# Exponentials issued behind the copies of B, two banks for the samples' transposes, and their decays loaded early, in a pooling and SSD step

## The chip, the cores and the metric

The kernel runs on one core of a Trainium2 chip. The metric is the time of one execution on the device, in microseconds (us). The core has five engines with a queue of instructions each: TensorE (PE, matmuls), VectorE (DVE), ScalarE (ACT), GpSimd (POOL) and SyncE (SP, which here issues nearly all DMAs). Each engine works through its own queue in order; what waits at the head of a queue holds all behind it. PEld is the loading of weights into PE, which overlaps its matmuls.

## The reference

One inference step of two layers, x = x + mixer(RMSNorm(x)), for a prompt of 1024 tokens and for eight sample requests of eight tokens with carried states. Layer 0 is a gated mixer of pooling windows, layer 1 a Mamba-2 mixer (SSD) with 32 heads of 64 in four groups, state size 128 and chunks of 128 tokens. The change is in layer 1, whose scan is:

```python
a = dt * A                                # per head
a_cum = cumsum(a, within the chunk of 128)
L = exp(where(causal, a_cum_i - a_cum_j, -inf))
CB = einsum('bcign,bcjgn->bcgij', C, B)   # B, C are shared by the 8 heads of a group
W = CB * L * dt
y_diag = einsum('bcgeij,bcjgep->bcigep', W, x)
decay_to_end = exp(a_cum_last - a_cum) * dt
chunk_states = einsum('bcjgn,bcgej,bcjgep->bcgepn', B, decay_to_end, x)
h = exp(a_cum_last) * h + chunk_states    # from chunk to chunk
y_off = einsum('bcign,bcgepn,bcgei->bcigep', C, h_before_chunk, exp(a_cum))
y = y_diag + y_off + D * x, gated by silu(z), normed, projected
```

## The kernel before

Everything is computed in fp32. A weight is split into a high and a low part (`whi`, `wlo`), an activation too, and three matmuls stand for one: high by high, low by high, high by low. The 1024 prompt tokens and the 64 sample tokens are worked in two halves h of 512 + 32 = 544 columns, and each product in two column halves of 272. So nearly all of PE's work is a row of 128x128 by 128x272 matmuls in `product` (line 172), 24 for a tile of 128 outputs of the input projections, into one of three PSUM banks `big`. ACT casts a weight to its high part (line 155); the low part comes by DMA or from DVE. Weights have two raw buffers and three of each part.

In layer 1 the four groups g of a half follow each other. While a group is worked, the projections, convolutions and gates of the same and of the next group supply the large matmuls among which its small ones are set. For a group:

- `ssd_common`: for each of four chunks c, PE transposes B (line 607) and multiplies C by B (608) into one bank of `tr` (two banks, used by many others too), and ACT copies both out: the product to `bs` (610), the transpose to `bt` (612).
- `sample_common`, `sample_states`: for the 32 sample tokens, eight small matmuls with C as the weight multiply the carried states (723, 32 rows each) into the bank `of`; ACT copies the result (725). For each quad q of four heads PE transposes it into `of` again (730; `of` is one bank), a DMA brings the decays `bEs` (734, one tile), and DVE multiplies the two into `ys` (737).
- `ssd`, for each quad q: for each chunk a DMA brings the decays `bA` (641, two tiles), POOL masks them (642), ACT takes four exponentials into `L` (646, four tiles), DVE multiplies them by `bs` (647); PE transposes x (650), DVE scales it to `xd` and `xs` (654), PE multiplies by `L` into `dg` (660). In the second half the state of the first comes in: PE multiplies it by C into `of` (674).
- `ssd_sample`: the same for the sample tokens, ending in a new state `hs` (775).
- the convolution of a tile: ACT copies u out of `big` (184), starts it (578), DVE adds three terms (580), ACT takes the tanh (592), DVE finishes it (593, 597).

When the first half is done, its closing norms are worked among the first group of the second half: PE sums squares over partitions (205), DVE scales (213), ACT takes the square root (214), DVE makes the reciprocal and one refining step (215 to 218), and PE spreads the result to all partitions (225).

The order on each engine is not the order of the code. The kernel is built with a scheduler that plays a timeline at build time and sets each engine's queue by when it believes inputs to be ready, within dependences; `tc.high_priority()` lifts a block in it. So an edit at one place can move rows on every queue.

Of the kernel before, what the change touches and what calls it, by code (L numbers as in the profile page):

```python
# [9 lines left out]
F32 = mybir.dt.float32  # L10
F32R = mybir.dt.float32r
AF = mybir.ActivationFunctionType
# [4 lines left out]
P = 128  # L17
# [8 lines left out]
NB = 4  # L26
LS = 8
SM = NB * LS
# [48 lines left out]
def pool_ssd_step(ctx, tc, xin, spool, sconv, sssm, w_pin, w_mix, w_pout, w_sin, w_dt, w_sout, params, consts,  # L77
                  y_out, pool_p, pool_s, conv_p, conv_s, ssm_p, ssm_s):
    nc = tc.nc
    V, S, G, PE = nc.vector, nc.scalar, nc.gpsimd, nc.tensor  # L80
# [4 lines left out]
    sp = ctx.enter_context(tc.tile_pool(name="sp", bufs=1))  # L85
    big = ctx.enter_context(tc.tile_pool(name="big", bufs=3, space=PSUM))
    sps = ctx.enter_context(tc.tile_pool(name="sps", bufs=1, space=PSUM))
# [385 lines left out]
    esd = [dp.tile([NH, SM], F32, name=f"esd{h}") for h in range(2)]  # L473
# [90 lines left out]
    def conv_part(h, act, g, j):  # L564
# [33 lines left out]
                               op0=ALU.add, op1=ALU.mult)  # L598
        return xpair[0] if j < 4 else o

    def ssd_common(B, C):

        out = []
        for c in range(NCH):
            cs = slice(c * Q, (c + 1) * Q)
            pb = sps.tile([P, 2, NS], F32, name="tr", bufs=2)
            PE.transpose(pb[:, 0], B[:, cs], ident)
            PE.matmul(pb[:, 1], B[:, cs], C[:, cs], start=True, stop=True)
            bs = sp.tile([P, 1, NS], F32, name="bs", bufs=NCH)
            S.copy(bs, pb[:, 1:])  # L610
            bt = sp.tile([P, NS], F32, name="bt", bufs=NCH)
            S.copy(bt, pb[:, 0])
            out.append((bs, bt))
        return out

    def heads(x):
        return x.rearrange("p (e d) -> p e d", e=4)
# [4 lines left out]
    def by_head(x, i):  # L622

        return x[:, i:i + 4, None].broadcast_to([x.shape[0], 4, HD])

    def ssd(h, g, q, x, ys, C, com, nat, cdb):
# [5 lines left out]
        for c0 in range(0, NCH, 2):  # L632
# [3 lines left out]
            for c in (c0, c0 + 1):  # L636
                cs = slice(c * Q, (c + 1) * Q)
                ci = c * NH + h0

                bA = sp.tile([P, 4, Q], F32, name="bA", bufs=2)  # L640
                nc.sync.dma_start(out=bA, in_=acd[h][c:c + 1, h0:h0 + 4].broadcast_to([P, 4, Q]))
                G.affine_select(out=bA, in_=bA, pattern=[[0, 4], [1, Q]], compare_op=ALU.is_ge, fill=-1e30, base=0,
                                channel_multiplier=-1)
                L = sp.tile([P, 4, Q], F32, name="L", bufs=4)
                for e in range(4):
                    S.activation(out=L[:, e], in_=bA[:, e], func=AF.Exp, bias=nat[:, 0, ci + e:ci + e + 1])  # L646
                V.tensor_tensor(out=L, in0=L, in1=com[c][0].broadcast_to([P, 4, Q]), op=ALU.mult)
                px = sps.tile([P, 2 * P], F32, name="tr", bufs=2)
                for k in range(2):
                    PE.transpose(px[:, k * P:(k + 1) * P], x[:, k, cs], ident)  # L650
                xd = sp.tile([P, 2 * P], F32, name="xd", bufs=2)
                xs = sp.tile([P, 2 * P], F32, name="xs", bufs=2)
                for k, x1 in enumerate((xd, xs)):
                    V.tensor_tensor(out=heads(x1), in0=heads(px), in1=by_head(nat[:, 1 + k], ci), op=ALU.mult)
                xds.append(xd)
                xss.append(xs)
                Ls.append(L)
# [5 lines left out]
            po = sps.tile([P, 2, 2 * Q], F32, name="of")  # L663
            bE = sp.tile([P, 2, 2 * Q], F32, name="bE")
            for n in range(2):
                c = c0 + n
                cs = slice(c * Q, (c + 1) * Q)
                ns = slice(n * Q, (n + 1) * Q)
                if hf is not None:
                    ev = ecd[h][c:c + 1, h0:h0 + 4].rearrange("c (k r) i -> c r k i", r=2)  # L670
# [41 lines left out]
    def sample_states(h, g, C):  # L712

        ss = slice(LP, T)
        states = []

        pn = sps.tile([P, 2, 2 * P], F32, name="of")
        for q in range(2):
            hs = sp.tile([P, NB, 2 * P], F32, name="hs", bufs=2)
            nc.sync.dma_start(out=hs, in_=sssm[h, g, q].rearrange("b p f -> p b f"))  # L720
            states.append(hs)
            for b in range(NB):
                PE.matmul(pn[b * SM:(b + 1) * SM, q], C[:, ss], hs[:, b], start=True, stop=True)
        yn = sp.tile([P, 2, 2 * P], F32, name="bE")
        S.copy(yn, pn)
        outs = []
        for q in range(2):
            po = sps.tile([P, 2, NB, SM + LS], F32, name="of")
            for k in range(2):
                PE.transpose(po[:, k].rearrange("p b i -> p (b i)")[:, :P], yn[:, q, k * P:(k + 1) * P], ident)  # L730
            bE = sp.tile([P, 2, SM], F32, name="bEs")
            ev = esd[h][None, g * 8 + q * 4:g * 8 + q * 4 + 4].rearrange("c (k r) i -> c r k i", r=2)
            for r in range(2):
                nc.sync.dma_start(out=bE[r * 64:(r + 1) * 64], in_=ev[:, r].broadcast_to([64, 2, SM]))
            ys = sp.tile([P, 2, T], F32, name="ys", bufs=2)

            V.tensor_tensor(out=by_seq(ys[:, :, ss]), in0=po[:, :, :, :LS], in1=by_seq(bE), op=ALU.mult)
            outs.append(ys)
        return states, outs
# [366 lines left out]
```

## Time and profile before

| | us |
|---|---|
| median of three runs | 1576.95 (1576.25 to 1577.57) |
| the profiled execution | 1577.91 |
| its span | 1575.8 |

The profiled execution is 0.96 us above the median; 2.11 us of it lie outside the span, which runs from the first recorded instruction to the last. PE is busy nearly all the time; the granted clock of TensorE is 0.994 of full on the mean. A reader looks for three things in such a profile: where PE stood idle and what ended it, in which windows its clock was below full, and what the other engines had in their queues at that time. Layer 1 starts in earnest at 703 us, where PE comes to the first group of the first half; the first group of the second half comes at 1129 us.

### The profile page before, as it was taken

What the parts mean: (1) busy time and instruction counts of PE and PEld (TensorE: products, weight loads), DVE (VectorE), ACT (ScalarE), POOL (GpSimd) and SP (SyncE); (2) the same over time, 40 slices, a digit from 0 to 9 for tenths busy, and PEclk for the clock granted to TensorE, in tenths of its full rate; (3) what the DMA queues carried; (4) which work ended last, traced back from release to release, by engine and by line L of the source; (5) the groups of instructions that cost most, each with busy time, mean ns of one, the idle gap of its engine ahead of it and who ended that gap; (6) DMA issues with size and microseconds to landing.
All of it is one profiled execution on the core that took longest, in us unless ns stands there. A gap on an engine that the chain in (4) does not pass through costs nothing.

```text
span 1575.8 us, 32628 instructions
## 1 busy us (share of the span) xinstructions
PE 1551.3 (98%) x12636; PEld 1514.5 (96%) x12636; DVE 1078.8 (68%) x2019; ACT 735.1 (47%) x1462; POOL 318.7 (20%) x516
## 2 busy tenths in 40 slices
PE   9999999999999999999999999999999999999996
PEld 8999999999999999998999999999999899999996
DVE  6787778865557576658666476577678864865757
ACT  5553433545343434355555554543645555535422
POOL 2200000003101011015432132222323521322310
PEclk9999999999999999999999999999999999999998
DMA  7856556758555556554846657656667576475563
GB/s 260 256 183 195 199 177 207 256 181 279 180 182 177 187 173 207 163 182 142 271 152 210 212 164 214 227 171 237 199 186 253 198 214 213 163 237 190 180 219 116
DMA packets 163210, 315.77 MB, mean 200 GB/s; under 512 B 33392, under 2 KB 71408, under 8 KB 163056
## 3 DMA queue, kind: packets, MB, share of 16 engines
q1 hardware_dynamic: 162768, 313.42, 61.8%
q8 instruction: 99, 1.62, 0.4%
q14 instruction: 55, 0.45, 0.1%
q10 hardware_dynamic: 288, 0.28, 0.1%
HBM read 262.47 MB, written 51.16 MB: 199 GB/s over the span
## 4 chain that ended last, share of the span: by engine, by line
PE 85%; DVE 5%; DMA 5%; ACT 1%; POOL 1%; issue 1%; SPq 1%; DVEq 0%; POOLq 0%; ACTq 0%
PE big L172 75%; PE dg L660 2%; PE stt L676 2%; PE of L674 1%; DVE win L580 1%; DMA bA<-acd 1%; DMA L<-in_w_sin_dram 1%; PE tr L650 1%; DMA bE<-ecd 1%; PE big L392 1%; DMA bEs<-esd 1%; PE stt L774 0%; DMA d<-d 0%; DMA low<-bA 0%; DVE X L888 0%
## 5 line engine op out<-in xcount | busy, mean ns | idle before, releaser
L172 PE MATMUL big<-ah,whi 128*128 128x272 f32 (+1 forms) x2304 | 667.1, 290 | 0.5 <-DVE X L428 0.5
L172 PE MATMUL big<-al,whi 128*128 128x272 f32 (+1 forms) x2304 | 666.9, 289 | 0.0
L172 PE MATMUL big<-ah,wlo 128*128 128x272 f32 (+1 forms) x2304 | 666.4, 289 | 0.0
L172 PEld LDWEIGHTS big<-ah,whi 128*128 128x128 f32 (+1 forms) x2304 | 432.1, 188 | 5.7 <-ACT bs L610 2.1
L172 PEld LDWEIGHTS big<-ah,wlo 128*128 128x128 f32 (+1 forms) x2304 | 432.7, 188 | 1.3 <-issue 0.4
L172 PEld LDWEIGHTS big<-al,whi 128*128 128x128 f32 (+1 forms) x2304 | 432.5, 188 | 1.0 <-issue 0.3
L155 ACT CAST whi<-raw 128x1024 fp32r<-128x1024 f32 (+1 forms) x228 | 237.8, 1043 | 361.1 <-PE big L172 272.6
L172 PE MATMUL big<-y,whi 128*128 128x272 f32 x2016 | 392.3, 291 | 2.2 <-DVE X L813 1.2
L172 PEld LDWEIGHTS big<-y,whi 128*128 128x128 f32 x2016 | 317.9, 188 | 5.6 <-DVE X L813 1.4
L172 PE MATMUL big<-y,wlo 128*128 128x272 f32 x1008 | 293.5, 291 | 0.0
L157 DVE TENSOR_TENSOR wlo<-raw,whi 128x1024 fp32r<-128x1024 f32 x112 | 138.6, 1238 | 87.8 <-ACT whi L155 86.3
L172 PEld LDWEIGHTS big<-y,wlo 128*128 128x128 f32 x1008 | 190.4, 189 | 0.7 <-issue 0.4
L580 DVE SCALAR_TENSOR_TENSOR win<-u,par,win 128x556 f32<-128x556 f32 x144 | 123.3, 857 | 43.7 <-ACT win L578 41.6
L646 ACT ACTIVATE L<-bA,nat 128x128 f32<-128x128 f32 x256 | 79.9, 390 | 47.3 <-PE dg L660 36.1
L141 ACT CAST bA<-L 128x512 fp32r<-128x512 f32 (+1 forms) x113 | 69.9, 619 | 62.7 <-DMA L<-in_w_sin_dram 34.6
L142 DVE TENSOR_TENSOR bA<-L,bA 128x512 fp32r<-128x512 f32 (+1 forms) x113 | 78.0, 691 | 27.5 <-ACT bA L141 25.0
L172 PE MATMUL big<-p,whi 128*128 128x272 f32 x512 | 96.7, 288 | 0.0
L172 PEld LDWEIGHTS big<-p,whi 128*128 128x128 f32 x512 | 80.3, 188 | 0.0
L331 POOL COPY uc<-u 128x15 f32<-128x15 f32 x30 | 22.3, 742 | 258.7 <-ACT u L184 169.2
L184 ACT COPY u<-big 128x272 f32<-128x272 f32 (+2 forms) x192 | 52.6, 309 | 46.0 <-PE big L172 35.3
L428 DVE TENSOR_TENSOR X<-X,big 128x272 f32<-128x272 f32 x128 | 54.5, 432 | 28.4 <-PE big L172 28.2
L172 PE MATMUL big<-p,wlo 128*128 128x272 f32 x256 | 73.6, 288 | 0.0
(228 smaller groups left out, 1941.6 us busy)
## 6 DMA issues: line engine op xcount, KB each, us to landing
wlo<-low SPq DMA_DIRECT2D x114, 512.0 KB, 3.5
raw<-in_w_sin_dram SPq DMA_DIRECT2D x80, 512.0 KB, 5.0
raw<-in_w_pin_dram SPq DMA_DIRECT2D x64, 512.0 KB, 4.0
low<-bA SPq DMA_DIRECT2D x112, 256.0 KB, 4.2
L<-in_w_sin_dram SPq DMA_DIRECT2D x80, 256.0 KB, 4.5
raw<-in_w_sout_dram SPq DMA_DIRECT2D x34, 512.0 KB, 4.7
raw<-in_w_pout_dram SPq DMA_DIRECT2D x32, 512.0 KB, 3.8
bA<-acd SPq DMA_DIRECT2D x64, 256.0 KB, 3.9
```

The costliest lines, as they stand in the source:

```text
L141: S.copy(hl, raw)
L142: V.tensor_tensor(out=hl, in0=raw, in1=hl, op=ALU.subtract)
L155: S.copy(hi[:, :cols], raw[:, :cols])
L157: V.tensor_tensor(out=lo[:, :cols], in0=raw[:, :cols], in1=hi[:, :cols], op=ALU.subtract)
L172: PE.matmul(ps, w[:, wsl], x[:, cols], start=first, stop=kt == kts - 1 and a == 2)
L184: S.copy(out, ps)
L331: G.tensor_copy(out=uc[:, m], in_=u[:, LP:LP + HALO])
L428: return lambda n, ps: V.tensor_tensor(out=half(X[d], n), in0=half(X[d], n), in1=ps, op=ALU.add)
L580: V.scalar_tensor_tensor(out=a[:, :n], in0=x[:, k:k + n], scalar=pcol(V_CW + ti * 4 + k), in1=a[:, :n], op0=ALU.mult, op1=ALU.add)
L646: S.activation(out=L[:, e], in_=bA[:, e], func=AF.Exp, bias=nat[:, 0, ci + e:ci + e + 1])
L660: PE.matmul(pd[e % 2 * HD:(e % 2 + 1) * HD, e // 2, n * Q:(n + 1) * Q], xds[n][:, e * HD:(e + 1) * HD], Ls[n][:, e], start=True, stop=True)
L676: PE.matmul(pst, com[c][1], xss[n], start=True, stop=True)
```

## The change

It has three parts. In `ssd_common` the last copy of a transposed B is kept, and the exponentials of `ssd` may be issued only behind it in ACT's queue: `tc.issue_after` gives the scheduler an order and adds no wait on a semaphore. In `sample_states` the second quad's transposes go to the bank `stt` instead of `of`. And the decays `bEs` have two tiles, one for each quad, and their four DMAs are issued at the head of the function, under high priority.

```diff
@@ -598,6 +598,8 @@
                                op0=ALU.add, op1=ALU.mult)
         return xpair[0] if j < 4 else o
 
+    copied = [None]
+
     def ssd_common(B, C):
 
         out = []
@@ -609,7 +611,7 @@
             bs = sp.tile([P, 1, NS], F32, name="bs", bufs=NCH)
             S.copy(bs, pb[:, 1:])
             bt = sp.tile([P, NS], F32, name="bt", bufs=NCH)
-            S.copy(bt, pb[:, 0])
+            copied[0] = S.copy(bt, pb[:, 0])
             out.append((bs, bt))
         return out
 
@@ -642,8 +644,10 @@
                 G.affine_select(out=bA, in_=bA, pattern=[[0, 4], [1, Q]], compare_op=ALU.is_ge, fill=-1e30, base=0,
                                 channel_multiplier=-1)
                 L = sp.tile([P, 4, Q], F32, name="L", bufs=4)
-                for e in range(4):
-                    S.activation(out=L[:, e], in_=bA[:, e], func=AF.Exp, bias=nat[:, 0, ci + e:ci + e + 1])
+
+                with tc.issue_after(copied[0].ins):
+                    for e in range(4):
+                        S.activation(out=L[:, e], in_=bA[:, e], func=AF.Exp, bias=nat[:, 0, ci + e:ci + e + 1])
                 V.tensor_tensor(out=L, in0=L, in1=com[c][0].broadcast_to([P, 4, Q]), op=ALU.mult)
                 px = sps.tile([P, 2 * P], F32, name="tr", bufs=2)
                 for k in range(2):
@@ -713,6 +717,12 @@
 
         ss = slice(LP, T)
         states = []
+        bEs = [sp.tile([P, 2, SM], F32, name="bEs", bufs=2) for q in range(2)]
+        with tc.high_priority():
+            for q in range(2):
+                ev = esd[h][None, g * 8 + q * 4:g * 8 + q * 4 + 4].rearrange("c (k r) i -> c r k i", r=2)
+                for r in range(2):
+                    nc.sync.dma_start(out=bEs[q][r * 64:(r + 1) * 64], in_=ev[:, r].broadcast_to([64, 2, SM]))
 
         pn = sps.tile([P, 2, 2 * P], F32, name="of")
         for q in range(2):
@@ -725,13 +735,10 @@
         S.copy(yn, pn)
         outs = []
         for q in range(2):
-            po = sps.tile([P, 2, NB, SM + LS], F32, name="of")
+            po = sps.tile([P, 2, NB, SM + LS], F32, name=("of", "stt")[q])
             for k in range(2):
                 PE.transpose(po[:, k].rearrange("p b i -> p (b i)")[:, :P], yn[:, q, k * P:(k + 1) * P], ident)
-            bE = sp.tile([P, 2, SM], F32, name="bEs")
-            ev = esd[h][None, g * 8 + q * 4:g * 8 + q * 4 + 4].rearrange("c (k r) i -> c r k i", r=2)
-            for r in range(2):
-                nc.sync.dma_start(out=bE[r * 64:(r + 1) * 64], in_=ev[:, r].broadcast_to([64, 2, SM]))
+            bE = bEs[q]
             ys = sp.tile([P, 2, T], F32, name="ys", bufs=2)
 
             V.tensor_tensor(out=by_seq(ys[:, :, ss]), in0=po[:, :, :, :LS], in1=by_seq(bE), op=ALU.mult)
```

No instruction is added or taken away on any engine; what changes is tiles and order. Up to the first group of the first half all queues are the same. Lines of the changed kernel are 2 to 10 higher from there on: the transposes of B are line 609, their copies 612 and 614, the exponentials 650, DVE's product 651, dg 664, the carried state's product 678, the samples' transposes 740 and DVE's reading of them 744.

In the first group of the first half ACT's queue was this, from the copy of u before a cast of weights on; `L_8964` and `L_8982` are tiles of exponentials, `tr_8818` and `tr_8825` the first two chunks' banks:

```order
L184 COPY u_8746<-big_8755 128x272
L750 ACTIVATE bAs_9026<-bAs_9026 128x32
L646 ACTIVATE L_8964<-bA_8959,nat_8495 128x128 x4
L155 CAST whi_9373<-raw_9371 128x1024
L184 COPY u_8746<-big_8781 128x240
L184 COPY u_8746<-big_8781 128x4x8
L610 COPY bs_8821<-tr_8818 128x128
L612 COPY bt_8823<-tr_8818 128x128
L646 ACTIVATE L_8982<-bA_8977,nat_8495 128x128 x4
L610 COPY bs_8828<-tr_8825 128x128
L612 COPY bt_8830<-tr_8825 128x128
```

and is now this, from the same copy of u on; the tanh (592) of the convolution `win0_8737` stood eleven rows further down before:

```order
L184 COPY u_8746<-big_8755 128x272
L592 ACTIVATE u_8673<-win0_8737 128x556
L155 CAST whi_9373<-raw_9371 128x1024
L184 COPY u_8746<-big_8781 128x240
L184 COPY u_8746<-big_8781 128x4x8
L612 COPY bs_8821<-tr_8818 128x128
L614 COPY bt_8823<-tr_8818 128x128
L612 COPY bs_8828<-tr_8825 128x128
L614 COPY bt_8830<-tr_8825 128x128
```

The four of exponentials ahead of the cast and the one between the two pairs of copies are gone from here; the tanh stands ahead of the cast. Four rows further ACT's queue is this:

```order
L614 COPY bt_8837<-tr_8832 128x128
L612 COPY bs_8842<-tr_8839 128x128
L614 COPY bt_8844<-tr_8839 128x128
L650 ACTIVATE L_8901<-bA_8896,nat_8495 128x128 x4
L650 ACTIVATE L_8919<-bA_8914,nat_8495 128x128 x3
L184 COPY u_9060<-big_9069 128x272
L650 ACTIVATE L_8919<-bA_8914,nat_8495 128x128
L592 ACTIVATE u_8746<-win1_8810 128x556
```

Behind the copy of the fourth chunk (`bt_8844`) stand the first two fours (`L_8901`, `L_8919`), which had been ahead of all of this before; `L_8964` and `L_8982` come ten rows later.

In the first group of the second half DVE read the samples' transposes (line 737) at two places:

```order
L647 TENSOR_TENSOR L_14707<-L_14707,bs_14561 128x512
L737 TENSOR_TENSOR ys_14604<-of_14598,bEs_14601 128x2x32
L702 TENSOR_SCALAR Bm_14572<-tr_14570,cst_75 128x128 x4
L709 TENSOR_TENSOR Ss_14581<-tr_14577,cst_75 128x32
L593 SCALAR_TENSOR_TENSOR p2_14445<-u_14449,win1_14513 128x512
L597 SCALAR_TENSOR_TENSOR p2_14445<-u_14449,win1_14513 128x32
L751 TENSOR_TENSOR bAs_14751<-bAs_14751,Ss_14581 128x32
L580 SCALAR_TENSOR_TENSOR win0_14849<-u_14785,par_76,win0_14849 128x556
L754 COPY xr_14757<-p2_14445 128x256
L580 SCALAR_TENSOR_TENSOR win0_14849<-u_14785,par_76,win0_14849 128x556
L737 TENSOR_TENSOR ys_14612<-of_14606,bEs_14609 128x2x32
```

and now reads them (line 744) in a row:

```order
L593 SCALAR_TENSOR_TENSOR p2_14445<-u_14376,win0_14440 128x512
L597 SCALAR_TENSOR_TENSOR p2_14445<-u_14376,win0_14440 128x32
L580 SCALAR_TENSOR_TENSOR win1_14513<-u_14449,par_76,win1_14513 128x556 x3
L744 TENSOR_TENSOR ys_14607<-of_14604,bEs_14583 128x2x32
L744 TENSOR_TENSOR ys_14612<-stt_14609,bEs_14584 128x2x32
L651 TENSOR_TENSOR L_14622<-L_14622,bs_14540 128x512
L706 TENSOR_SCALAR Bm_14572<-tr_14570,cst_75 128x128 x4
L651 TENSOR_TENSOR L_14640<-L_14640,bs_14547 128x512
L713 TENSOR_TENSOR Ss_14581<-tr_14577,cst_75 128x32
```

The readings stand together, ahead of the products with `bs` and of the sample's other work, each with its own bank and tile.

At the closing norm of the first half DVE had a convolution's steps (line 580) and the norm's in this order:

```order
L580 SCALAR_TENSOR_TENSOR win0_15785<-u_15721,par_76,win0_15785 128x556
L213 TENSOR_SCALAR dts_15674<-tr_15669 128x136
L580 SCALAR_TENSOR_TENSOR win0_15785<-u_15721,par_76,win0_15785 128x556
L215 RECIPROCAL dts_15674<-dts_15674 128x136
L580 SCALAR_TENSOR_TENSOR win0_15785<-u_15721,par_76,win0_15785 128x556
L216 SCALAR_TENSOR_TENSOR dts_15674<-dts_15674 128x136
L217 TENSOR_TENSOR dts_15674<-dts_15674 128x136
L218 SCALAR_TENSOR_TENSOR dts_15674<-dts_15674 128x136
```

and has them now in this one:

```order
L213 TENSOR_SCALAR dts_15674<-tr_15669 128x136
L580 SCALAR_TENSOR_TENSOR win0_15785<-u_15721,par_76,win0_15785 128x556
L215 RECIPROCAL dts_15674<-dts_15674 128x136
L580 SCALAR_TENSOR_TENSOR win0_15785<-u_15721,par_76,win0_15785 128x556
L216 SCALAR_TENSOR_TENSOR dts_15674<-dts_15674 128x136
L580 SCALAR_TENSOR_TENSOR win0_15785<-u_15721,par_76,win0_15785 128x556
L217 TENSOR_TENSOR dts_15674<-dts_15674 128x136
L218 SCALAR_TENSOR_TENSOR dts_15674<-dts_15674 128x136
```

The norm's first step stands ahead of the three convolution steps instead of behind the first.

## Rows read from the trace of the kernel before

**Rows 1.** The page, busy time and share of the span of each engine

```profile
PE 1551.3 (98%) x12636; PEld 1514.5 (96%) x12636; DVE 1078.8 (68%) x2019; ACT 735.1 (47%) x1462; POOL 318.7 (20%) x516
```

**Rows 2.** Waits of PE: what waited, for what; us in total, times, longest

```profile
PE tr L607 <- ACT bt L612: 2.4, 1, 2.4
...
PE of L674 <- DVE ys L737: 1.5, 2, 1.1
...
PE tr L225 <- DVE dts L218: 1.3, 1, 1.3
...
PE big L172 <- DVE X L813: 1.2, 1, 1.2
...
PE dg L660 <- DVE xd L654: 0.3, 1, 0.3
```

**Rows 3.** Windows of 1 us: length, PE, PEld, DVE, ACT, POOL, PE clock, DMA

```profile
713.00:714.00 1.00, 1.00 (x7) 1.00 (x6) 1.00 (x2) 1.00 (x4) 1.00 (x2) 0.50 0.93 367
...
716.00:717.00 1.00, 1.00 (x8) 1.00 (x8) 1.00 (x2) 0.15 (x1) 1.00 (x2) 0.83 0.04 8
```

**Rows 4.** Timeline of ACT: start, duration, operation, count, idle time before and its end

```profile
699.55 1.28 ACT L646 ACTIVATE L<-bA,nat 128x128 f32<-128x128 f32 x4 [3.96 <-POOL bA L642]
700.74 1.03 ACT L155 CAST whi<-raw 128x1024 fp32r<-128x1024 f32 x1
...
704.20 0.85 ACT L578 ACTIVATE win<-u,par 128x556 f32<-128x556 f32 x1
...
708.69 1.28 ACT L646 ACTIVATE L<-bA,nat 128x128 f32<-128x128 f32 x4 [3.24 <-POOL bA L642]
...
711.30 0.27 ACT L612 COPY bt<-tr 128x128 f32<-128x128 f32 x1
```

**Rows 5.** Timelines of PE and DVE in the same stretch

```profile
698.65 0.29 PE L172 MATMUL big<-ah,wlo 128*128 128x272 f32 x1
698.78 0.29 PE L172 MATMUL big<-ah,whi 128*128 128x272 f32 x1
...
705.16 2.46 DVE L580 SCALAR_TENSOR_TENSOR win<-u,par,win 128x556 f32<-128x556 f32 x3 [0.84 <-ACT win L578]
```

**Rows 6.** Windows from the first transpose of B to the next large matmul

```profile
703.67:706.12 2.45, 2.45 (x25) 1.21 (x23) 1.17 (x3) 1.76 (x8) 0.00 (x0) 1.00 0.62 164
813.25:815.01 1.76, 1.76 (x24) 1.06 (x22) 0.61 (x3) 1.68 (x6) 0.53 (x3) 1.00 0.34 79
```

**Rows 7.** Timelines: DVE in the first half, PE in the second half's first group

```profile
725.07 0.23 DVE L737 TENSOR_TENSOR ys<-of,bEs 128x64 f32<-128x64 f32 x1 [1.55 <-DMA bEs<-esd]
...
1142.84 0.44 PE L730 MATMUL of<-cst,bE 128*128 128x128 f32 x2 [0.51 <-DVE ys L737]
...
1148.41 0.71 PE L674 MATMUL of<-p,hf 128*128 128x128 f32 x4 [1.08 <-DVE ys L737]
```

**Rows 8.** Timelines of DVE and ACT at the closing norm of the first half

```profile
1226.12 0.80 DVE L580 SCALAR_TENSOR_TENSOR win<-u,par,win 128x556 f32<-128x556 f32 x1 [4.53 <-ACT win L578]
1226.84 0.29 DVE L213 TENSOR_SCALAR dts<-tr 128x136 f32<-128x136 f32 x1
...
1226.94 1.28 ACT L214 ACT_TABLE_LOAD   x1
1228.24 0.32 ACT L214 ACTIVATE dts<-dts 128x136 f32<-128x136 f32 x1
...
1228.95 0.99 DVE L215 RECIPROCAL dts<-dts 128x136 f32<-128x136 f32 x1
```

**Rows 9.** Timelines of DVE, ACT and PE in the first half's second group

```profile
814.92 1.98 DVE L647 TENSOR_TENSOR L<-L,bs 128x512 f32<-128x512 f32 x2 [1.15 <-ACT bs L610]
...
818.52 0.28 ACT L612 COPY bt<-tr 128x128 f32<-128x128 f32 x1
...
828.65 1.09 PE L660 MATMUL dg<-L,xd 128*64 128x128 f32 x16
...
830.13 1.26 ACT L646 ACTIVATE L<-bA,nat 128x128 f32<-128x128 f32 x4
```

## The prediction

> **What bounds the kernel now.** I read the page's busy line first: TensorE (PE) is busy 1551.3 us, 98% of a span of 1575.8 us, VectorE (DVE) 68%, ScalarE (ACT) 47%, GpSimd (POOL) 20% [rows 1]. The kernel is a queue of matmuls, and nothing changes their number. So a change of order can gain only what PE loses between matmuls, by a slower clock, or by small matmuls set in badly. The second view is PE's waits by what ended them [rows 2]. In the stretch that the change touches, layer 1 from 703 us on, they sum to some 8 us. The largest is one wait of 2.4 us, of the third transpose of B (L607) for the copy of B on ACT (L612); it happens in one group of eight. The third view is the windows of 1 us behind that wait [rows 3]: the granted clock falls from 1.00 to 0.50, which is 1.2 instead of 2.4 GHz, for three windows, from 713 to 716 us, and is 0.83 in the fourth. The time lost is 3 x 0.50 + 0.17, about 1.7 us. So this wait costs 4.1 us, not 2.4.
>
> **What the change does, part by part.** The durations are of the profiled execution (1577.91 us: its span and 2.11 us around it); it stands 0.96 us above the median of 1576.95, and I carry that difference over unchanged.
>
> *Term A, the first group of the first half.* ACT works through its queue in order. Before, the exponentials of four chunks stand ahead of the copies of B, and ACT waits for them: 3.96 us before 699.55 and 3.24 us before 708.69, both for POOL's mask of the decays [rows 4]. Behind the last of them stand a cast of weights, two copies of u and the copies of B. PE's third transpose needs one of two banks of `tr`, which only those copies free; it starts as the copy of 711.30 ends. After the change the exponentials stand behind the last copy of B. I walk ACT's new queue with the same durations [rows 4, 5]. Before, 3.46 us lie between the cast at 700.74 and the convolution's start at 704.20, a four of exponentials (1.28) among them; without it 2.2. The cast can now begin when PE leaves the old weights, 698.7 [rows 5], so the start begins at 700.9 and ends at 701.8, and three steps on DVE (2.46) end at 704.3. Tanh over as many columns as the start takes at most its 0.85. Cast, copies of u and the first pair of copies of B took 1.6 before (from the exponentials' end, 709.97, to 711.57): 706.8, and the second pair at most 0.5 more, 707.3. PE starts its small matmuls at 703.67 as before, is through them at 705.4 (term A2), and comes to the third transpose 20 large matmuls later, each 0.125 us behind the last (698.65 and 698.78 in [rows 5]), at 707.9. The margin is 0.6 us and the wait nil; with DVE's steps some tenths longer it is used up. That gives 2.37, the 1.7 of the clock, and the 0.3 that PE waits for xd some 15 us later, which comes late for the same reason [rows 2]: **4.4 us** (2.4 to 4.4).
>
> *Term A2, the small matmuls.* The same 12 small matmuls (two transposes, two of C times B, eight with the carried states, L723; each stands twice in the trace) take 2.45 us in the first group and 1.76 us in the next, where they stand in another order [rows 6]. The first group of the second half has the dear order as well. In the new order both have the cheap one: 2 x 0.69 = **1.4 us** (0 to 1.4).
>
> *Term B, two banks and early decays (first group of the second half).* Before, both samples' transposes use the one bank `of`. The second waits 0.51 us until DVE has read the first, and the matmul with the carried state (L674) 1.08 us for the second's reading [rows 7]. DVE's read in turn stands behind other work or a DMA: in the first half it waited 1.55 us for the decays, which have a single tile [rows 7]. With a bank and a tile for each, PE makes all four transposes in a row and DVE reads both in a row, 0.2 us each; `of` is free again some 20 matmuls (2.5 us) before the next user. **1.6 us** gone (0.5 to 1.6). In the next group what is left of the L674 row, 1.5 less 1.1 [rows 2], goes the same way: **0.4**. What it costs: the four DMAs of the decays leave SyncE's queue earlier, at the head of the group. They wait there for the tile of the group before, and the loads of weights behind them wait with them. Those stand behind a wait for weight buffers anyway, so I cost it at nothing; without that cover it is at most the 1.55 us of [rows 7] for each of eight groups.
>
> *Term C, the closing of the first half.* PE waits 1.3 us for dts (L218) [rows 2]. The chain from the sums (L205) over DVE, the square root on ACT and back is set by the order on DVE: L213 stands behind a convolution step that started only at 1226.12, and the reciprocal behind two more [rows 8]. The new order has L213 ahead of all three steps. The chain is then 0.3 + 1.28 + 0.32, the reciprocal and, at most as long as it, two steps at 0.99 each, and three small steps of 0.3: 5.8 us, up to 1.1 more if small steps meet work on POOL. Between L205 and L225 stand 57 large matmuls (7.1 us), where 53 stood. L205 itself must not come before POOL's sums are ready: from the norm ahead of it 238 rows of PE stand before it instead of 235, so it comes no earlier against them. I take **1.0** (0 to 1.3).
>
> The chain holds a load of ACT's function table, which the trace has at 1.28 us, with the square root 0.02 us behind it [rows 8]. The Trainium skill (ScalarE: Activation LUTs, "What ACT_TABLE_LOAD costs") gives about 1.28 us for the load, which agrees, and a drain of about 1.38 us on top, which this row doesn't show. By that rule the new chain would be, as an estimate, 7.2 us and would not fit; term C would be nil and the time 1 us more.
>
> *Term E, what the new wait costs.* In every group eight exponentials (1.26 us a four [rows 9]) now stand between the last copy of B and DVE's product of them with bs. Before, they were done by then; the two products of the second group began at 814.92 [rows 9]. There the last copy ends at 818.8, so two fours end at about 821.3 plus what ACT has between; DVE's two products, about 1 us each in that row (1.98 for the two), follow. The matmul that needs them (dg, L660) starts at 828.65 [rows 9], and the new order puts dg nine large matmuls (1.1 us) later. By my walk DVE is done with xd 1.0 to 1.6 us before PE comes to dg. Queued behind the exponentials on ACT are the copy of u (first half of a product, one of three banks of `big`) and the casts of weights; two banks of `big` remain, 24 matmuls or 3 us each, against a delay of about 2.4 us. So in most groups all is covered; thin margins in eight groups will open some small waits. I take **1.5 us** lost (0 to 8; the lower end is the eight groups' full cover, the upper 1 us a group).
>
> The wait at 1200 us for X (L813, 1.2 us [rows 2]) and the sample's hs beside it I leave as they are, since nothing ahead of them moves by more than a few matmuls. The sum: 4.4 + 1.4 + 1.6 + 0.4 + 1.0 - 1.5 = **7.3 us**. 1577.91 - 7.3 = 1570.6 for a profiled execution, 1569.7 for the median.
>
> **The rivals.** (1) *The gain is eaten group by group.* The exponentials were ahead of need; now copies, exponentials, DVE's product and dg are one chain. If each group loses 0.7 to 1 us there, term E is 6 to 8 us and the net 0.8 to 2.8: 1574 to 1576. For it: margins of 1.0 to 1.6 us were walked with durations that spread (DVE's products of exponentials are 0.99 us each in [rows 9] beside work on POOL, a convolution step 0.80 in [rows 8] without). Against: dg moved back in the new order by about what is needed. (2) *Slower: a long wait at dg in the steady groups.* If the chain is late by more than about 2.4 us beyond its margin, PE waits as it does today at L607, and the clock may drop behind each wait: 4.1 us in each of the other six groups, 24.6 us, less the other terms, 8.8: about 1593. It decides when the two fours or their masks (POOL's, which kept ACT waiting 3.24 and 3.96 us in [rows 4]) come 3.5 to 4 us later than walked. Against: the trace has waits of 1.1 to 1.3 us [rows 2] after which the clock stays whole. (3) *The wait at L607 only changes its releaser.* Tanh, the cast and the copies of u still stand ahead of the copies of B; if the three DVE steps run late, 1 to 2.4 us stay and the clock drops too: terms A2, B and C alone remain, 4.4 less 1.5, about 1574.
>
> Weighed against the trace is also what the clock does. It fell only after the longest wait and not after the waits of 1.1 to 1.3 us [rows 2, 3]. The Trainium skill (TensorE: Matmul & The Clock Gate, "Part 1: The HAM clock gate") says that the throttled state is the default and that activity releases it, so small matmuls before the wait could count as much as the wait does. As a rival (4) worked from rows: if the split row of small matmuls, not the wait, brings the drop, the 1.7 us stay, and the time is 1571.4.
>
> **How the numbers follow.** Forecast (with rival 4, which lies inside its range) 0.70, rival 1 0.14, rival 3 0.09, rival 2 0.07. The forecast's own range is 1566.5 to 1573.5: all terms at their best, with the wait for X gone too, are 4.4 + 1.4 + 1.6 + 0.4 + 1.3 + 1.2 = 10.3 (1566.7), and with A at 2.4, A2 at 0.7 and C at nil 3.6 (1573.4). To hold 8 in 10 it reaches into rivals 1 and 3, to 1576.2. A measurement of this kernel can tell 0.2%, 3.15 us, from no change: faster is below 1573.8, slower above 1580.1. Faster takes nearly all of the forecast and a little of rival 3 (0.72), within 0.2% the rest of 1 and 3 (0.21), slower rival 2 (0.07).
>
> **What would show it.** Right: no PE wait at the transposes of B (now L609), the clock at 1.00 from 700 to 730 us, no wait at L678 and L740 near 1140 to 1150, less than 0.5 us at L225 near 1230, and waits at dg (L664) and for u that sum to under 3 us. Wrong: a wait over 1 us at dg or for a copy of u in several groups, or a clock of 0.50 at another place; idle time of PE in layer 1 that does not fall below 5 us would show that the order moved the waits and removed none.

## The result and the profile after

The changed kernel is slower: 1590.06 us (median of five, 1589.59 to 1593.95) against 1577.57 us, a ratio of 1.0082 (95% interval 1.0071 to 1.0093). The forecast was 1569.7 and a range up to 1576.2. The profiled execution took 1589.59 us, with a span of 1587.8.

The first thing to read is that the gain forecast for the first group did come. The transposes of B no longer wait, and the small matmuls beside them stand in the cheap order; they take 1.75 us, as in the shorter row of [rows 6]. Windows of the kernel after: the small matmuls of the first group, and the 8 us from 703 us on, in which the old wait would have fallen. The columns are those of [rows 3].

```profile
702.09:703.84 1.75, 1.75 (x24) 1.05 (x22) 0.80 (x2) 1.75 (x7) 0.39 (x2) 1.00 1.14 353
...
703.00:711.00 8.00, 8.00 (x74) 7.42 (x67) 4.84 (x11) 6.39 (x23) 7.23 (x12) 1.00 0.68 217
```

PE is busy in all 8 us, and the clock is 1.00 and stays there up to 742 us. The same large matmul that stood at 723.17 us before stands at 716.77 now; 1.6 us of that lead existed before layer 1, so 4.8 us were won within 20 us. Then it is lost again. PE's waits of the kernel after, in the columns of [rows 2]:

```profile
PE of L678 <- DVE hf L686: 5.2, 5, 1.8
PE tr L654 <- DVE xs L658: 2.9, 2, 2.0
...
PE tr L225 <- DVE dts L218: 2.1, 2, 1.9
...
PE dg L775 <- DVE ys L692: 1.7, 3, 1.3
...
PE tr L205 <- POOL ssq L251: 1.2, 1, 1.2
...
PE stt L781 <- DVE hf L686: 0.9, 1, 0.9
...
PE of L678 <- ACT hf L683: 0.7, 1, 0.7
```

None of these is the matmul dg (L664), at which I looked for the damage. They are the carried state (L678, L781), a transpose of x whose bank `tr` DVE has not emptied (L654) and a sample's product (L775), and nearly all wait for small steps on DVE. Taken over the same large matmuls of both kernels, the stretches of layer 1 are (us; the starts are those of the kernel before, the first one at 706 us, behind the small matmuls of the first group; e9 is an experiment below):

```
stretch from  first group  819    922    1024   1125   1240   1347   1441   sum
before        113.1        102.6  102.2  101.5  114.9  106.6   94.5  109.6  845.0
after         114.7        105.0  102.1  103.1  113.5  110.8   97.4  112.4  859.0
e9            108.6        102.7  102.1  102.6  109.1  104.5   94.2  109.6  833.4
```

The loss of 14.0 us is what six stretches lose, less what two gain. Over all eight PE's recorded waits rise from 8.2 to 19.1 us and the time lost to a lower clock from 1.7 to 3.4; 0.7 come off by the small matmuls of the second half's first group. Some 2 us are neither in waits nor in the clock, and I can't say more of these.

Why DVE is late stands in the queues. Timelines of ACT, SyncE, POOL and DVE in the first group of the second half (start, duration, operation; in brackets the idle time before and what ended it):

```profile
1137.48 2.46 ACT L650 ACTIVATE L<-bA,nat 128x128 f32<-128x128 f32 x8
...
1150.11 2.52 ACT L650 ACTIVATE L<-bA,nat 128x128 f32<-128x128 f32 x8 [1.36 <-POOL bA L644]
...
1156.23 1.28 ACT L650 ACTIVATE L<-bA,nat 128x128 f32<-128x128 f32 x4 [1.45 <-POOL bA L644]
...
1160.12 1.28 ACT L650 ACTIVATE L<-bA,nat 128x128 f32<-128x128 f32 x4 [2.33 <-POOL bA L644]
...
1167.46 1.28 ACT L650 ACTIVATE L<-bA,nat 128x128 f32<-128x128 f32 x4 [2.42 <-POOL bA L644]
```

```profile
1139.18 3.04 SPq L725 DMA_DIRECT2D bEs<-esd  x4
...
1145.36 6.41 SPq L643 DMA_DIRECT2D bA<-acd  x3
...
1149.38 0.70 POOL L644 TENSOR_SCALAR_AFFINE_SELECT bA<-bA 128x512 f32<-128x512 f32 x1 [5.79 <-DMA bA<-acd]
...
1161.44 0.69 DVE L651 TENSOR_TENSOR L<-L,bs 128x512 f32<-128x512 f32 x1 [2.14 <-ACT L L650]
1162.05 0.42 DVE L686 TENSOR_TENSOR hf<-hf,stt 128x256 f32<-128x256 f32 x1
```

```profile
1162.52 0.71 PE L678 MATMUL of<-p,hf 128*128 128x128 f32 x4 [1.12 <-DVE hf L686]
```

These are the turns of two tiles. The first two fours of exponentials run right behind the copies (1137.48), because two tiles bA lay masked. Only their end frees the tiles. The loads of the next two stand on SyncE behind other DMAs, the four early decays among them (3.04 us), and leave at 1145.36; POOL masks the first at 1149.38; the next exponentials start at 1150.11, 12.6 us after the first. Over the eight groups the third four follows the first after 7.7 to 13.5 us. The later turns of this group take 6 to 9 us each, and ACT waits for a mask at each of the later rows shown. At the sixth four (1160.12) DVE has waited 2.14 us at the product for the exponentials (L651), the next state `hf` stands behind that product in its queue though it doesn't need it, and PE waits for `hf`.

Before, in six of the eight groups four fours lay finished in the tiles L and two more were masked when the group began, so the turns were made ahead of need. In the first group of either half two lay finished at its start, and four by the last copy of B. Exponentials and masks of the kernel before, for the group whose transposes start at 813.25 us [rows 6]:

```profile
750.93 1.28 ACT L646 ACTIVATE L<-bA,nat 128x128 f32<-128x128 f32 x4 [0.41 <-PE dg L660]
752.36 1.28 ACT L646 ACTIVATE L<-bA,nat 128x128 f32<-128x128 f32 x4
763.14 2.45 ACT L646 ACTIVATE L<-bA,nat 128x128 f32<-128x128 f32 x8 [1.75 <-PE dg L660]
...
770.74 0.64 POOL L642 TENSOR_SCALAR_AFFINE_SELECT bA<-bA 128x512 f32<-128x512 f32 x1 [2.81 <-DMA bA<-acd]
772.06 0.64 POOL L642 TENSOR_SCALAR_AFFINE_SELECT bA<-bA 128x512 f32<-128x512 f32 x1 [0.69 <-DMA bA<-acd]
```

### The profile page after: what moved, and what is told of

Read it like the earlier page. It is cut to its first block, busy times and chain, and to the rows that moved or that the text cites. A ratio compares the mean times of both kernels' runs of the same rounds, so it can differ in the third digit from the quotient of the medians.

```text
span 1587.8 us, 32602 instructions
## 1 busy us (share of the span) xinstructions
PE 1552.1 (98%) x12636; PEld 1514.3 (95%) x12636; DVE 1066.5 (67%) x2019; ACT 736.4 (46%) x1462; POOL 309.3 (19%) x516
## 4 chain that ended last, share of the span: by engine, by line
PE 78%; DVE 6%; DMA 6%; issue 4%; ACT 3%; POOL 2%; SPq 1%; POOLq 0%; DVEq 0%; ACTq 0%
PE big L172 70%; DMA bA<-acd 2%; ACT L L650 1%; PE dg L664 1%; PE stt L680 1%; PE of L678 1%; POOL bA L644 1%; DMA bE<-ecd 1%; DMA L<-in_w_sin_dram 1%; PE big L392 1%; DVE win L580 1%; ACT whi L155 1%; POOL ssq L251 0%; PE of L733 0%; PE stt L781 0%
## 5 line engine op out<-in xcount | busy, mean ns | idle before, releaser
L580 DVE SCALAR_TENSOR_TENSOR win<-u,par,win 128x556 f32<-128x556 f32 x144 | 118.9, 825 | 60.7 <-ACT win L578 57.2
L650 ACT ACTIVATE L<-bA,nat 128x128 f32<-128x128 f32 x256 | 80.7, 392 | 53.7 <-POOL bA L644 50.9
L644 POOL TENSOR_SCALAR_AFFINE_SELECT bA<-bA 128x512 f32<-128x512 f32 x64 | 46.0, 721 | 150.4 <-DMA bA<-acd 128.4
```

The costliest lines, as they stand in the source:

```text
L580: V.scalar_tensor_tensor(out=a[:, :n], in0=x[:, k:k + n], scalar=pcol(V_CW + ti * 4 + k), in1=a[:, :n], op0=ALU.mult, op1=ALU.add)
```

## The experiments

Each kernel was timed beside the kernel before on the same chip; ratios are to that kernel, with 95% intervals. Line numbers are those of the kernel after or up to three lower; e6 and e8 have those of the kernel before.

**Which part costs.** First the parts alone. e1 is the change to `ssd_common` and `ssd` only, e2 that to `sample_states` only. e3 has all of the change, but holds the exponentials in the first group of the first half alone:

```diff
-                with tc.issue_after(copied[0].ins):
+                with tc.issue_after(copied[0].ins) if (h, g) == (0, 0) else nullcontext():
```

> Only the exponentials are issued behind the copies of B; banks and decays as before. Theory 1 (the lead is lost: before, four fours of exponentials of a group lay ready in the tiles L some 60 us ahead of it; behind the copies all eight fours must be made inside the group, two at a time, since bA has two tiles and each turn of DMA, mask and exponentials takes 6 us or more): as slow as the changed kernel, 1586 to 1593. Theory 2 (the samples' part is to blame: the bank stt is shared with the chunk states, and the decays' DMAs at the head of SyncE's queue hold the weights): 1570 to 1574, since the wait at L607 goes and nothing is lost. Theory 3 (any new order of the scheduler costs some us by chance): between, with waits at other places than in the changed kernel.

Measured: 1585.73 us, 1.0045 (1.0028 to 1.0061).

> Only the two banks and the early decays; exponentials as before. Theory 1: 1574 to 1578: the wait at the second transposes and at the carried state near 1142 and 1148 us goes (1.6 us), the wait of 2.4 us for a copy of B stays or moves. Theory 2: 1586 to 1593, with PE waiting at stt or for weights. Theory 3: 1576 to 1584.

Measured: 1572.59 us, 0.9962 (0.9949 to 0.9975).

> The changed kernel with the exponentials held behind the copies in the first group of the first half alone, where the wait of 2.4 us was. Theory 1: the six or seven other groups get their lead back; what the changed kernel loses from 760 us on (about 8 us) is gone, what it loses in the first group itself (waits of 1.95 and 0.85 us near 740 us and 3.4 us by the clock) stays: 1577 to 1583. Theory 2: 1586 to 1593. Theory 3: no telling, 1575 to 1590.

Measured: 1573.65 us, 0.9969 (0.9959 to 0.998).

The order of the exponentials costs, the samples' part gains: theory 2 falls. e2 and e3 came out below what theory 1 gave; held in one group only, the exponentials cost the kernel nothing that shows beside e2. e1 is slower than before by 7 us, e2 faster by 6, and both together are slower by 12.5: they don't add up. The parts meet on SyncE. ACT and SyncE of e1 in the first group of the second half:

```profile
1139.88 2.45 ACT L650 ACTIVATE L<-bA,nat 128x128 f32<-128x128 f32 x8
...
1147.64 1.28 ACT L650 ACTIVATE L<-bA,nat 128x128 f32<-128x128 f32 x4 [2.40 <-POOL bA L644]
```

```profile
1143.04 1.02 SPq L643 DMA_DIRECT2D bA<-acd  x2
```

With the samples' part as before, the loads of bA leave 3.2 us after the first exponentials start, and not 7.9. The third four follows the first after 7.8 us here, and after 7.0 to 7.8 us in all eight groups. So the samples' part, which gains by itself, lengthens the first turn where the exponentials are held; and held exponentials cost 7 us even with the shorter turn.

e2 also shows what the second bank does not do. A wait of PE there, in the first group of the second half:

```profile
1139.83 0.71 PE L677 MATMUL of<-p,hf 128*128 128x128 f32 x4 [1.05 <-DVE ys L743]
```

The second quad has a bank of its own, and the carried state still waits for `of`, as in [rows 7]: it is the first quad's reading on DVE that comes late. The samples' part gains elsewhere. In e2 the first group has two waits of 1.15 and 1.41 us instead of the one of 2.37, and no drop of the clock follows.

**Whether the turn of the tiles is the cause.** If it is, more tiles for masked decays must mend it with the exponentials still behind the copies. e4 writes the exponentials in place and has six tiles bA, in the memory of two bA and four L:

```diff
-                bA = sp.tile([P, 4, Q], F32, name="bA", bufs=2)
+                bA = sp.tile([P, 4, Q], F32, name="bA", bufs=6)
...
-                L = sp.tile([P, 4, Q], F32, name="L", bufs=4)
+                L = bA
```

e9 and e10 keep both tiles and shift the memory: four bA and two L, three bA and three L. (The stash of low parts in layer 0 uses tiles of these names; it keeps six.)

> The changed kernel with the exponentials written in place: bA has six tiles, L none, in the same memory. Masks can run six tiles ahead of the copies, so only the exponentials themselves are made inside the group. Theory 1: the turn of DMA and mask is off the path; most of the 12 us come back: 1571 to 1578, and ACT's idle time ahead of the exponentials (50.9 us for POOL's masks in the changed kernel) falls below 15. Theory 2: 1586 to 1593, nothing gained. Theory 3: no telling; the wait for masks falls, the time stays above 1582.

Measured: 1566.9 us, 0.9926 (0.9912 to 0.994).

> The changed kernel with four tiles bA and two L instead of two and four, in the same memory; exponentials not in place. Refined theory 1 (behind the copies only masked decays are a lead, so the number of tiles bA decides: two in the changed kernel, six in the kernel in place): four masked fours at a group's start are enough for its first two pairs, the time falls from 1590 to 1566 to 1574 and ACT's idle time for masks (50.9 us) to below 30. Theory 3 (the kernel in place only met a lucky order): 1577 to 1592.

Measured: 1565.79 us, 0.9925 (0.9911 to 0.994).

> The changed kernel with three tiles bA and three L. Refined theory 1: between the two, a lead of three: 1572 to 1584, ACT's idle time for masks between that of the changed kernel (50.9 us) and that of four tiles. Theory 3: no order among two, three, four and six tiles.

Measured: 1569.94 us, 0.9952 (0.9937 to 0.9967).

With the exponentials held in all of them, two, three and four tiles give 1590, 1570 and 1566 us, and six in place 1567; all three experiments came out below the ranges that theory 1 gave. That is the cause shown by its size: what behind the copies counts as a lead is masked decays. The exponentials of e9 in the same group as above:

```profile
1127.38 2.53 ACT L650 ACTIVATE L<-bA,nat 128x128 f32<-128x128 f32 x8
...
1138.72 2.45 ACT L650 ACTIVATE L<-bA,nat 128x128 f32<-128x128 f32 x8
...
1150.10 2.44 ACT L650 ACTIVATE L<-bA,nat 128x128 f32<-128x128 f32 x8
```

No brackets: ACT never waited for a mask here. But the third four follows the first after 11.3 us here too. So the exponentials are not sooner in their group than in the kernel after; what is gone is that ACT, and DVE behind it, stand waiting for them. DVE's product with `bs` in the kernels before, after and e9, one row each (busy us, mean ns; then DVE's idle time ahead of it and what ended it):

```profile
L647 DVE TENSOR_TENSOR L<-L,bs 128x512 f32<-128x512 f32 x64 | 53.0, 846 | 18.2 <-ACT bs L610 14.4 <-ACT L L646 3.4
```

```profile
L651 DVE TENSOR_TENSOR L<-L,bs 128x512 f32<-128x512 f32 x64 | 48.2, 754 | 34.0 <-ACT L L650 33.3
```

```profile
L651 DVE TENSOR_TENSOR L<-L,bs 128x512 f32<-128x512 f32 x64 | 50.4, 798 | 1.4 <-ACT L L650 0.9
```

DVE waits 33.3 us for exponentials in the kernel after, 3.4 before and 0.9 in e9. The sum is not the price: it is 42.9 us in e1, which loses less. Over the whole run, the groups of exponentials of the kernels before, after, e10 and e9, one row each (busy us, mean ns; then ACT's idle time ahead of them and what ended it):

```profile
L646 ACT ACTIVATE L<-bA,nat 128x128 f32<-128x128 f32 x256 | 79.9, 390 | 47.3 <-PE dg L660 36.1 <-POOL bA L642 11.2
```

```profile
L650 ACT ACTIVATE L<-bA,nat 128x128 f32<-128x128 f32 x256 | 80.7, 392 | 53.7 <-POOL bA L644 50.9 <-PE dg L664 2.7
```

```profile
L650 ACT ACTIVATE L<-bA,nat 128x128 f32<-128x128 f32 x256 | 80.7, 395 | 18.9 <-PE dg L664 10.2 <-POOL bA L644 5.9 <-POOL u L572 2.8
```

```profile
L650 ACT ACTIVATE L<-bA,nat 128x128 f32<-128x128 f32 x256 | 79.8, 398 | 8.8 <-PE dg L664 8.5
```

The releaser tells the story, not the sum of idle time: before, ACT waited for dg, that is for a free tile L, far ahead of need; after, it waited for masks, 50.9 us; in e9 for none. In e4 it waited 21.4 us for masks, more than the 15 I had written.

Of the scan's matmuls none is left in the list of PE's waits of e9. From layer 1 up to the last closing it has the wait for X, which stands in [rows 2] too, and one for y:

```profile
PE big L172 <- DVE X L820: 1.5, 2, 1.1
...
PE big L172 <- DVE y L281: 0.3, 1, 0.3
```

**Whether the tiles alone do it.** e5 and e6 have the six tiles in place with the exponentials free to run ahead, e5 with the samples' part, e6 without; e12 is e9 with the exponentials free.

> The six tiles in place, two banks and early decays, but the exponentials free to run ahead of the copies again. With six tiles exponentials may run up to six fours ahead. If holding them behind the copies was itself a gain that the lack of tiles ate up (theory 1 as far as it goes), this is slower than the kernel in place with the order kept (1566.9): 1569 to 1573, with a wait of 1 us or more in the first group. If the gain of that kernel is its six tiles and nothing else (theory 1b), it is as fast or faster: 1564 to 1568.

Measured: 1577.29 us, 1.0002 (0.9991 to 1.0012).

> The kernel before with the exponentials in place in six tiles; no part of the change. Theory 1: the wait of 2.4 us at L607 and the drop of the clock behind it may stay, since exponentials that wait for masks can again stand ahead of the copies: 1572 to 1577. Theory 1b (six tiles are the whole gain): 1565 to 1569.

Measured: 1576.52 us, 0.9992 (0.9984 to 1.0001).

> Four tiles bA, two L, two banks and early decays, but the exponentials free to run ahead of the copies. If both are needed (the order on ACT and a lead of masks), it is slower than the same with the order, 1565.8: 1570 to 1578, as the kernel in six tiles without the order was (1577.3 against 1566.9). If four tiles of bA are the whole gain: 1564 to 1568.

Measured: 1569.18 us, 0.9938 (0.9921 to 0.9955).

The order of the change gains 10 us with six tiles in place. With four and two it gains 3.4 us, less than I had put down (1570 to 1578), and the intervals of e9 and e12 overlap, so that isn't told apart. Nor do four tiles bA gain much by themselves: e12 differs from e2 by the tiles alone and is 3.4 us faster, and these intervals overlap too. With the exponentials held, the same tiles gain 24 us. e6 came where theory 1 had it, though without a wait at copies of B. e5 lands above both its cases. Its waits are not at copies of B but at the samples' reading, at hs and at X, and the clock falls at the last of these; why the free order does worse with six tiles in place than with four and two stays open.

Each of these kernels has an order of its own on every queue, and that moves the time too: the five whose exponentials are free and whose tiles or banks differ (e2, e5, e6, e8 and e12) lie between 1569 and 1577 us. So a difference of a few us between two kernels can be a luckier order; the 20 and more between two tiles and three or four, in one direction three times, can hardly be.

**How much lead is needed, and SyncE's part.** e8 takes half of the tiles L from the kernel before; e7 is the changed kernel with the loads of bA on another queue:

```diff
-                nc.sync.dma_start(out=bA, in_=acd[h][c:c + 1, h0:h0 + 4].broadcast_to([P, 4, Q]))
+                nc.scalar.dma_start(out=bA, in_=acd[h][c:c + 1, h0:h0 + 4].broadcast_to([P, 4, Q]))
```

> The kernel before with two tiles L instead of four (the stash of low parts keeps two tiles of its own); no part of the change. It takes half of the lead away without any order put on ACT. Theory 1: four fours of lead become two; waits at the carried state (L674) and at transposes for DVE appear in several groups, 1581 to 1590. If the lead does not matter, 1576 to 1580.

Measured: 1574.05 us, 0.9978 (0.9969 to 0.9988).

> The changed kernel with the loads of the decays bA issued from ACT's queue instead of SyncE's. In the changed kernel the second pair's loads leave 3.5 us after the exponentials that free the tiles, behind other DMAs on SyncE. If that queue is what makes a turn long (theory 1c), the turn shortens by some 3 us and the time falls to 1576 to 1584. If the turn is long by the DMA itself (4.2 us to landing), POOL's masks and the exponentials (theory 1), it stays at 1586 to 1593; ACT's queue pays for issuing 64 loads.

Measured: 1585.38 us, 1.0045 (1.003 to 1.006).

e8 missed: two tiles L less cost nothing. So theory 1 as I had first put it, a lead of four finished fours that must not be halved, is too strong. In six of its eight groups e8 still holds four chunks at the start, two finished and two masked; the changed kernel holds two masked in every group, e10 three and e9 four. Read so, two are too few, and three or four are enough. e7 fell between its two cases and wins back 4.7 us of the 12.5: SyncE's queue is part of the turn, and the smaller one. The third four of that group follows the first after 6.8 us there (12.6 above), about as in e1, and e7 takes what e1 takes:

```profile
1142.80 1.58 ACT L650 ACTIVATE L<-bA,nat 128x128 f32<-128x128 f32 x5
...
1149.62 1.28 ACT L650 ACTIVATE L<-bA,nat 128x128 f32<-128x128 f32 x4 [1.01 <-POOL bA L644]
```

The DMA to its landing (3.5 to 5.4 us in that stretch), the mask (0.64) and the exponentials (1.28) are what is left of a turn, and these only more tiles can hide.

**The samples' part beside the mended order.** e11 is e4 without it.

> Exponentials in place in six tiles and held behind the copies, but the samples' part as before (one bank, one tile of decays). If the samples' part adds its 1.6 to 2 us to the gain: 1568 to 1571, with waits at L678 or L730 for DVE's reading near 1140 us. If the order of the exponentials does it alone: 1566 to 1568.

Measured: 1568.44 us, 0.9943 (0.9929 to 0.9956). It differs from e4 by 1.5 us, the size I had put on term B, but the two intervals overlap, so this isn't told apart.

The best kernel is e9, the change with four tiles bA and two L: it beats the kernel before by 0.75% and the changed kernel by 24 us.

## Why the prediction was wrong

**Term A was right.** The wait at L607, the drop of the clock behind it and the wait for xd are gone; 4.8 us were won up to 717 us, against 5.1 predicted (4.4 and half of A2), of which the 0.3 for xd lay further on. The walk of ACT's queue had the second pair of copies end at 707.3, which is 705.7 in a run that is 1.6 us ahead; it ended at 704.2, and the third transpose came at 706.45. The margin was 2.2 us, not 0.6. Rival 3 is refuted with it.

**Term A2 was right**: 1.75 us instead of 2.45.

**Term B was right in part.** The wait at the second transposes is gone and PE makes all four in a row, and at the first quad's carried state there is no wait in the kernel after. But e2 and e3 have the same banks and tiles and a wait of 1.05 us there. So the second bank is not what removed it; it was the place of DVE's reading in its queue. The 0.4 us of the next group did not come: 0.3 are still waited there. And the part's cost was not nothing. No wait for weights is recorded in layer 1, but the loads of bA left later, and with the samples' part the held exponentials cost 12.5 us instead of e1's 7, its own gain included.

**Term C was wrong in sign.** I predicted 1.0 us won. PE waits 1.19 us at L205 and 1.85 at L225, 3.0 instead of 1.3. DVE does make L213 first:

```profile
1225.06 0.30 DVE L213 TENSOR_SCALAR dts<-tr 128x136 f32<-128x136 f32 x1 [1.75 <-PE tr L205]
...
1229.57 1.00 DVE L215 RECIPROCAL dts<-dts 128x136 f32<-128x136 f32 x1 [1.38 <-ACT dts L214]
```

```profile
1227.26 0.64 ACT L828 ACTIVATE ssq<-p 128x544 f32<-128x544 f32 x1
1227.92 1.28 ACT L214 ACT_TABLE_LOAD   x1
1229.22 0.32 ACT L214 ACTIVATE dts<-dts 128x136 f32<-128x136 f32 x1
```

The timelines of DVE and ACT show the fault. I had added up the chain's steps as if ACT took the square root at once. L213 ends at 1225.36 and the table load starts at 1227.92, behind 2.6 us of other work on ACT (a cast, copies of u, a convolution's start, a square). The step that failed is "the chain is then 0.3 + 1.28 + 0.32 ...": it walked one queue and not the other. And L205 does come early against POOL's sums, which end at 1224.50; the count of 238 rows instead of 235 was no measure of it. The load begins 0.02 us behind the square, and the square root 0.02 us behind the load, as in [rows 8]. The drain of 1.38 us that the Trainium skill adds to a load ("ScalarE: Activation LUTs", "What ACT_TABLE_LOAD costs") is not seen in these rows either.

**Term E is the step that decided.** "I take 1.5 us lost" and "in most groups all is covered" rested on a walk that ended at the first dg of a group, and there it held: PE has no recorded wait at dg (L664). I didn't walk on to the third chunk. Its exponentials need a tile bA that the first pair frees only behind the copies, and then a place on SyncE, a DMA, a mask. The trace of before had this price in [rows 4], where ACT waited 3.24 and 3.96 us for masks; I read these rows as what held the copies back and not as what a turn of the tiles costs. I also named SyncE's queue for the weights behind the decays' loads and not for bA's. The size by the profiles: 14.0 us were lost from 706 us on, while the other terms won 5.1 us in that stretch (A 4.4, A2 0.7, B 1.7, C -1.7), so term E came to about 19 us instead of 1.5. With four tiles (e9) the exponentials held in the same way gain 12.5 us on the kernel before, more than the 7.3 forecast. So of the other terms only C had a share in the loss, and e9, in which DVE has the old order at the closing, has no wait there.

**Rival 2 was the one that came**, at about its time (1593 against 1590), with 0.07. Its condition, fours or masks that come 3.5 to 4 us later than walked, was not met by the first two fours, which ran right behind the copies; it was met by the third, which the walk left out. Its place and its price were not met: the waits are not at dg but where small steps stand behind L651 in DVE's queue, and they are many of 0.2 to 2.0 us rather than six of 2.4 with a drop of the clock each. That its time was met is luck. Within the scan the clock fell once, in the first group. Rival 1 named the right chain, with an upper end of 1 us a group; it was nearer to 2.4 (the 19 us over eight groups).

**The clock** fell in the kernel after 0.9 us behind the wait of 1.95 us at L654, the longest of its scan; windows of 1 us:

```profile
742.00:743.00 1.00, 0.97 (x7) 0.76 (x5) 1.00 (x2) 0.00 (x0) 0.64 (x1) 0.68 0.18 52
743.00:744.00 1.00, 0.35 (x2) 0.22 (x2) 1.00 (x2) 0.00 (x0) 0.00 (x0) 0.50 0.62 194
...
748.00:749.00 1.00, 1.00 (x6) 1.00 (x6) 1.00 (x3) 0.00 (x0) 0.00 (x0) 0.50 0.10 21
```

It is 0.50, 1.2 GHz, up to 749 us and costs 3.4 us at most (0.85 us of that stretch are a wait). Rival 4, by which the row of small matmuls brings the drop, falls for the row alone: the kernel before has the same split row at 1128.76 us (2.45 us) with the clock at 1.00 from there to 1136 us, and e2 has it in its first group, with no drop behind it. Whether the row and the wait together brought the drop is not told apart.

## What to carry to other kernels

An order that holds a step back also holds back every tile that the step would have freed. Before such an order is added, count what lies ready at the point where it is let go, and walk on until the tiles have turned once: here two tiles lay ready for eight uses, the first turn took 12.6 us in the group shown, through ACT's, SyncE's and POOL's queues and a DMA, and the price came out on small steps queued behind the late one. Where memory is short, tiles are worth most ahead of the step that is held back: the same six tiles, split four to two instead of two to four, turned a loss of 0.8% into a gain of 0.75%.

When a chain is summed up from the steps of one engine, the other engines' queues must be walked too; the square root that stood behind 2.6 us of unrelated work on ACT undid a step that was moved forward rightly on DVE.

## What the hardware showed

The length of a wait does not decide on the clock by itself. The clock fell behind a wait of 1.95 us in the kernel after, behind one of 1.81 us in e1, and in e3 (at 1204 us) and e8 (at 1198 us) behind one of 1.25 us, with a shorter one some us ahead of it. It stayed at 1.00 behind one of 1.82 us at 1273 us in the kernel after, one of 1.97 us in e8, and two of 2.06 and 2.12 us in e7. So the prediction's reading, that waits of 1.1 to 1.3 us leave the clock whole, held for the kernel before and not in general. What tells these apart the runs here don't show.
